# RWKV's recurrence on the whole array for two heads at once, compression weights in two halves, and another order of layer B's score products

## The chip, the cores and the metric

The kernel runs on one core of one Trainium2 chip. The metric is the device time of one execution in microseconds. "TensorE", "VectorE", "ScalarE", "GpSimd" and "SyncE" are the core's engines; the profile calls them PE (and PEld for its weight loads), DVE, ACT, POOL and SP.

## The reference, cut to what matters

Two blocks over a sequence of 256 tokens of width 2048, all in fp32. The first block projects the normed input, mixes it in two ways (NSA attention and RWKV7), gates and projects back; the second block is a differential attention layer (layer A) and a gated linear attention layer (layer B). The three places that the change touches:

```python
def rwkv7_mixer(feat, ...):            # 16 heads of 64
    def step(state, inp):
        r_t, w_t, k_t, v_t, a_t, b_t = inp
        sa = jnp.einsum('bhij,bhj->bhi', state, a_t)
        state = (state * w_t[:, :, None, :] + sa[..., None] * b_t[:, :, None, :]
                 + v_t[..., None] * k_t[:, :, None, :])
        return state, jnp.einsum('bhij,bhj->bhi', state, r_t)
...
# in nsa_mixer: keys and values of 32-token windows, through two small matrices
kc = compress(k_cmp, cmp_pos_k, cmp_k_w1, cmp_k_w2)
vc = compress(v_cmp, cmp_pos_v, cmp_v_w1, cmp_v_w2)
...
def _gla(h, ...):                      # layer B, 4 heads, chunks of 64
    def step(state, xs):
        qi, ki, vi, ti = xs
        state = jnp.exp(ti)[..., None] * state + jnp.einsum('bchk,bchv->bhkv', ki, vi)
        return state, jnp.einsum('bchk,bhkv->bchv', qi, state)
```

## The kernel before, in words

**Big products.** `gemm` (line 476) multiplies a group of weight columns with the activations. Weights come in tiles of 512 KB (`wr`, four buffers) over SyncE's queue; `weights` (line 454) lets ScalarE make the upper half of each (`wh`) and VectorE the lower half (`wl`), both in fp32r, and TensorE runs three passes (wh with the upper and the lower half of x, wl with the upper half). These steps fill most of TensorE's time. The names of the accumulators tell the group: acc_rk, acc_v, acc_kk, acc_za, acc_q, acc_Bv and so on.

**Order.** Nothing is issued as it is written. Every operation goes to a recorder, and `Plan.schedule` (line 279) makes each engine's order ahead of time from a cost model: an operation is taken when what it needs is done and a buffer of its tag is free, and among those that can start the one that is recorded first is taken (weights first of all). Buffers of a tag go out in the order of first use. `Plan.run` (line 377) books the time, with an extra for TensorE when the array's shape changes. The order on each engine is then fixed; on the chip each engine goes through its list and waits by semaphores. All loads are issued by SyncE's queue, in order.

**RWKV.** `rwkv_group` (line 795) does four heads at once, so four groups g = 0..3; `rwkv_heads` (line 765) calls it after the products rk and v of that group. The 256 tokens are four chunks c of 64. AV and BK hold the scaled vectors, AB their products with the causal masks. The inverse of a triangular 32x32 block per head and half chunk is made by GpSimd on `blocks`, through DRAM (db, dy, dx), and completed by small products pT, pY, pX into M1. M2 holds the values in its own half of the partitions and the state in the other half. The recurrence is the loop over c near the end: pU = M1 times M2, copied by ScalarE to AVt; pS = BKt times AVt, from which VectorE makes the next state in M2; yp = AB times AVt, for c > 0 plus RT times M2. Chunk c uses partitions 0 to 63 or 64 to 127 by its parity (`own`), the state comes from the other half (`oth`). Each is one product a head:

```python
for h in range(4):
    mm(pu[own, h], M1[rows, h, c], M2[rows, c, h], ...)
```

so each writes 64 partitions, and the array is used as 128\*64 (or 64\*64 for c = 0 and for RT). An fp32 product is two MATMUL instructions in the profile. yp of all chunks stays in one PSUM bank until the group norm reads it (`bn_stats`).

**Compression.** `compress` (line 1137) is a generator that `weights` moves on by one step after each weight tile of rk2 and v2: for keys and values (kind) it loads w1 in four parts of 512 KB (tag t4, shared with many others) and runs eight products per part into ph, with 32 output partitions each, four column places in turn (128\*32).

**NSA.** `nsa_group` (line 1187) keeps probabilities of the compressed keys in pc4, two tiles a group of four heads.

**Layer B.** `gla_scores` (line 1570) makes, per head, decayed keys d (tile kd) and k2, scaled queries q1 and q2, and the scores in pB: per j of two, six products of 64 output partitions (128\*64) and then one of 128 (128\*128) from k2 and q2. The second half of k2 is a copy that GpSimd makes. VectorE also does the rest of the scaling, the upper and lower halves ATB of the scores and the wl tiles of the big product Bv that runs meanwhile (`layer_b`, line 1461).

Of the kernel before, what the change touches and what calls it, by code (L numbers as in the profile page):

```python
# [423 lines left out]
class Kernel:  # L424
# [8 lines left out]
    BUFS = {"t1": 6, "t2": 10, "t4": 5, "tiny": 24, "rtiny": 12, "rt4": 4, "rt2": 2, "rt1": 2, "rt8": 1}  # L433
# [361 lines left out]
    def rwkv_group(self, g, twd, fr, fk, fv):  # L795
# [82 lines left out]
        RT = self.sb(f"RT{g}", [128, 2, 4, 64], "rt2")  # L878
        for i in range(2):
            for o in range(2):  # L880
                S.activation(RT[hf(o), :, i:4:2, :].rearrange("p c j t -> p j c t"), AV[hf(i), :, 1 - o:4:2, 2, :], AF.Copy)

# [6 lines left out]
        AB = (self.work if g % 2 else self.big).tile([128, 4, 4, 2, 64], F32, name=f"AB{g}", tag="ml")  # L889
        for j in range(2):  # L890

            ps = [self.ps(f"pA{g}{2 * j + i}", (128, 4, 128)) for i in range(2)]
            for c in range(4):
                for i in range(2):
                    mm(ps[i][:, c], BK[hf(i), j, c].rearrange("p a t -> p (a t)"), AV[hf(i), j, c, c % 2:3:2 - c % 2, :],
                       start=(c == 0), stop=True, skip_group_check=True)
            for i in range(2):
                V.tensor_tensor(AB[:, 2 * j + i].rearrange("p c k t -> p c (k t)"), ps[i],
                                cst[:, None, C_SI:C_SI + 128].to_broadcast([128, 4, 128]), op=OP.mult)
# [5 lines left out]
        db = self.dram.tile([4, 4, 2, 32, 32], F32, name=f"db{g}")  # L905
        for q, c1, d in quads:
            nc.sync.dma_start(db[q].rearrange("h c s t -> s h c t"), AB[qp(q), :, c1:4:2, 0, 32 * d:32 * d + 32])
        Y, X = self.blocks[gp, 0], self.blocks[gp, 1]
        nc.sync.dma_start(Y, db.rearrange("q h c s t -> (q h c) s t"))
# [9 lines left out]
        dy = self.dram.tile([4, 4, 2, 32, 32], F32, name=f"dy{g}")  # L919
        nc.sync.dma_start(dy.rearrange("q h c s t -> (q h c) s t"), Y)  # L920
        dx = self.dram.tile([4, 4, 2, 32, 32], F32, name=f"dx{g}")
        nc.sync.dma_start(dx.rearrange("q h c s t -> (q h c) s t"), X)

# [17 lines left out]
        for c, c1, c2, h in units:  # L941
            mm(pv[hf(c1), c2, h], AB[hf(1 - c1), h, c, 0], AVt[hf(1 - c1), c, h], start=(c2 == 0 and h == 0), stop=True, skip_group_check=True)
# [5 lines left out]
        X = self.sb(f"X{g}", [128, 4, 2, 32], "t1", bufs=2)  # L948
        for q, c1, d in quads:
            nc.sync.dma_start(M1[qp(q), :, c1:4:2, 32 * d:32 * d + 32], dy[q].rearrange("h c s t -> s h c t"))  # L950
            if d == 0:
                nc.sync.dma_start(X[qp(q)], dx[q].rearrange("h c s t -> s h c t"))
            else:
                G.memset(M1[qp(q), :, c1:4:2, 0:32], 0.0)
# [3 lines left out]
        for c, c1, c2, h in units:  # L958
            lo, hi = qp(2 * c1), qp(2 * c1 + 1)
            mm(pt[hi, c2, h], AB[lo, h, c, 0, 32:64], X[lo, h, c2], start=(c2 == 0 and h == 0), stop=True, skip_group_check=True)  # L960
# [3 lines left out]
        for c, c1, c2, h in units:  # L964
            lo, hi = qp(2 * c1), qp(2 * c1 + 1)
            mm(py[lo, c2, h], Tm[hi, c2, h], M1[hi, h, c, 32:64], start=(c2 == 0 and h == 0), stop=True, skip_group_check=True)
        for c1 in range(2):
            S.activation(M1[qp(2 * c1), :, c1:4:2, 32:64].rearrange("p h c t -> p c h t"), py[qp(2 * c1)], AF.Copy)
        pt = self.ps(f"pX{g}", (128, 2, 4, 64))
        for c, c1, c2, h in units:  # L970
            mm(pt[hf(1 - c1), c2, h], AVt[hf(c1), c, h], M1[hf(c1), h, c], start=(c2 == 0 and h == 0), stop=True, skip_group_check=True)
        for c1 in range(2):
            S.activation(M1[hf(1 - c1), :, c1:4:2].rearrange("p h c t -> p c h t"), pt[hf(1 - c1)], AF.Copy)


        yp = self.ps(f"yp{g}", U3)
        for c in range(4):
            c1, c2 = c % 2, c // 2
            own, oth = hf(c1), hf(1 - c1)
            rows = slice(0, 128) if c else own  # L980
            pu = self.ps(f"pU{g}{c}", (128, 4, 64))
            for h in range(4):
                mm(pu[own, h], M1[rows, h, c], M2[rows, c, h], start=(h == 0), stop=True, skip_group_check=True)
            S.activation(AVt[own, c], pu[own], AF.Copy)
            if c < 3:
                pS = self.ps(f"pS{g}{c}", (128, 4, 64))
                for h in range(4):
                    mm(pS[own, h], BKt[:, c, h], AVt[:, c, h], start=(h == 0), stop=True, skip_group_check=True)
                pc = PC[own, c].rearrange("p j i -> p (j i)")[:, :, None].to_broadcast([64, 4, 64])
                Sn = M2[own, c + 1]  # L990
                if c:
                    V.tensor_tensor(Sn, pS[own], M2[oth, c], op=OP.add)
                    V.tensor_tensor(Sn, Sn, pc, op=OP.mult)
                else:
                    V.tensor_tensor(Sn, pS[own], pc, op=OP.mult)
            for h in range(4):
                o = yp[own, c2 * 4 + h]
# [694 lines left out]
```

## Time and profile before

| | us |
|---|---|
| runs of the kernel before | 1483.18, 1483.45, 1488.77 |
| median | 1483.45 |
| the profiled execution, its own time | 1483.21 |
| its span, first to last instruction | 1481.4 |
| mean granted TensorE clock | 0.995 |

The profile is of one execution. A row of a timeline gives the start, the duration, the engine and what is written and read; instructions of one kind in a row are put together with their count. The ends of matmuls are modelled and they overlap, so the text goes by distances from start to start. "Idle before <- releaser" says for how long the engine stood before this instruction and what ended that.

### The profile page before, as it was taken

Reading aid. Unit: us, or ns where it says so; the run is one execution under the profiler, and the core shown is the slowest. Engines: PE = TensorE matmul, PEld = TensorE weight load, DVE = VectorE, ACT = ScalarE, POOL = GpSimd, SP = SyncE. Lnnn points to the kernel's source line nnn. Section 1 sums busy time; section 2 is a strip of 40 time slices with the busy share of each in tenths; the row PEclk is TensorE's granted clock in tenths of the full one; section 3 lists DMA queues with packets and bytes.
Section 4 is the critical chain, followed back from the end, with each engine's and each line's share of the span. In section 5 each row is a group of like instructions: output and inputs, shape, how many; then the busy total and the mean of one; then the engine's idle time right before and its main releaser. Section 6 shows DMA issues by size and latency. Waiting matters only on the chain.

```text
span 1481.4 us, 24543 instructions
## 1 busy us (share of the span) xinstructions
PE 1454.8 (98%) x9437; PEld 1278.9 (86%) x9437; DVE 967.3 (65%) x1678; ACT 768.4 (52%) x1269; POOL 316.4 (21%) x402
## 2 busy tenths in 40 slices
PE   8999999999999999999999999999999998999998
PEld 8988889989999988788888888788888897988887
DVE  5876575575857754876767676656765567565554
ACT  6542345344545544757575757554544473455532
POOL 0258846615600000030404050100100001000000
PEclk9999999999999999999999999999999999999999
DMA  9545434636524567665556566556665553655564
GB/s 334 182 131 198 160 97 139 194 104 183 156 82 148 165 218 228 212 190 174 182 171 185 167 180 215 174 186 197 205 208 186 173 172 110 222 174 185 185 213 128
DMA packets 91957, 263.42 MB, mean 178 GB/s; under 512 B 19960, under 2 KB 26512, under 8 KB 91840
## 3 DMA queue, kind: packets, MB, share of 16 engines
q1 hardware_dynamic: 91840, 261.86, 56.6%
q8 instruction: 74, 1.21, 0.3%
q14 instruction: 43, 0.35, 0.1%
HBM read 253.92 MB, written 7.90 MB: 177 GB/s over the span
## 4 chain that ended last, share of the span: by engine, by line
PE 90%; DVE 6%; issue 1%; ACT 1%; DMA 1%; POOL 1%; SPq 0%; DVEq 0%; ACTq 0%
PE acc_Bo L277 6%; PE acc_Aq L277 6%; PE acc_Ao L277 6%; PE acc_o L277 6%; PE acc_Ak L277 6%; PE acc_Av L277 6%; PE acc_rk L277 6%; PE acc_Bg L277 6%; PE acc_Ag L277 5%; PE acc_Bv L277 5%; PE acc_zb L277 3%; PE acc_Bq L277 3%; PE acc_q L277 3%; PE acc_Bk L277 3%; PE acc_v L277 3%; PE acc_za L277 2%
## 5 line engine op out<-in xcount | busy, mean ns | idle before, releaser
L277 PE MATMUL acc_rk<-xp,wh_rk 128*128 128x256 f32 x512 | 96.7, 289 | 1.3 <-ACT wh_rk L277 1.3
L277 PE MATMUL acc_Bo<-mBp,wh_Bo 128*128 128x512 f32 x256 | 89.7, 396 | 0.0
L277 POOL TENSOR_TENSOR bt<-blocks 32x30 f32<-32x30 f32 (+14 forms) x120 | 87.5, 729 | 9.0
L277 PE MATMUL acc_Ao<-mAp,wh_Ao 128*128 128x512 f32 x256 | 89.3, 395 | 0.0
L277 PE MATMUL acc_Bv<-wh_Bv,xBp 128*128 128x412 f32 (+1 forms) x320 | 88.3, 355 | 0.0
L277 PE MATMUL acc_Aq<-wh_Aq,xAp 128*128 128x512 f32 x256 | 86.0, 407 | 0.7 <-ACT xAp L277 0.7
L277 PEld LDWEIGHTS acc_rk<-xp,wh_rk 128*128 128x128 f32 x512 | 80.6, 193 | 4.9 <-issue 2.6
L277 POOL TENSOR_TENSOR blocks<-blocks,bt 32x30 f32<-32x30 f32 (+14 forms) x120 | 80.8, 673 | 9.3
L277 PE MATMUL acc_Ag<-wh_Ag,xAp 128*128 128x512 f32 x256 | 81.6, 395 | 0.0
L277 PE MATMUL acc_Ak<-wh_Ak,xAp 128*128 128x512 f32 x256 | 80.8, 392 | 0.0
L277 PE MATMUL acc_Av<-wh_Av,xAp 128*128 128x512 f32 x256 | 80.8, 392 | 0.0
L277 PE MATMUL acc_Bg<-wh_Bg,xBp 128*128 128x512 f32 x256 | 80.5, 393 | 0.0
L277 PE MATMUL acc_o<-wh_o,mp 128*128 128x512 f32 x256 | 79.8, 392 | 0.0
L277 PE MATMUL acc_rk<-xp,wl_rk 128*128 128x256 f32 x256 | 72.9, 286 | 0.5 <-DVE wl_rk L277 0.5
L277 PE MATMUL acc_Bo<-mBp,wl_Bo 128*128 128x256 f32 x256 | 71.1, 280 | 0.0
L277 PE MATMUL acc_Ao<-mAp,wl_Ao 128*128 128x256 f32 x256 | 70.9, 279 | 0.0
L277 DVE TENSOR_TENSOR wl_o<-wr_o,wh_o 128x1024 fp32r<-128x1024 f32 x32 | 39.2, 1225 | 38.2 <-ACT wh_o L277 38.0
L277 DVE TENSOR_TENSOR wl_Bo<-wr_Bo,wh_Bo 128x1024 fp32r<-128x1024 f32 x32 | 39.2, 1224 | 36.0 <-ACT wh_Bo L277 36.0
L277 DVE TENSOR_TENSOR wl_Bg<-wr_Bg,wh_Bg 128x1024 fp32r<-128x1024 f32 x32 | 39.2, 1225 | 33.9 <-ACT wh_Bg L277 33.9
L277 ACT ACTIVATE wh_Bo<-wr_Bo 128x1024 fp32r<-128x1024 f32 x32 | 34.0, 1062 | 51.8 <-PE acc_Bo L277 48.5
L277 PEld LDWEIGHTS acc_Bv<-wh_Bv,xBp 128*128 128x128 f32 x320 | 60.1, 190 | 0.9
L277 DVE TENSOR_TENSOR wl_rk<-wr_rk,wh_rk 128x1024 fp32r<-128x1024 f32 (+1 forms) x33 | 41.5, 1260 | 29.0 <-ACT wh_rk L277 29.0
(731 smaller groups left out, 4426.4 us busy)
## 6 DMA issues: line engine op xcount, KB each, us to landing
wr_o<-w SPq DMA_DIRECT2D x32, 512.0 KB, 3.6
wr_Aq<-w SPq DMA_DIRECT2D x32, 512.0 KB, 3.7
wr_Ak<-w SPq DMA_DIRECT2D x32, 512.0 KB, 3.7
wr_Av<-w SPq DMA_DIRECT2D x32, 512.0 KB, 3.9
wr_Ag<-w SPq DMA_DIRECT2D x32, 512.0 KB, 3.6
wr_Ao<-w SPq DMA_DIRECT2D x32, 512.0 KB, 3.8
wr_Bg<-w SPq DMA_DIRECT2D x32, 512.0 KB, 4.3
wr_Bo<-w SPq DMA_DIRECT2D x32, 512.0 KB, 3.9
```

The costliest lines, as they stand in the source:

```text
L277: op.issued = getattr(getattr(self.nc, op.eng), op.method)(*op.args, **op.kw)
```

## The change

RWKV: M1, X, AB and the DRAM tiles get an order with the heads of a chunk side by side (`at(c)` puts chunks of one parity together), so that two heads are one operand of 128 columns. pU, pS and yp become two products a chunk instead of four, with all 128 rows and 128 output partitions; of each result the two diagonal 64x64 blocks (`own2`) are taken and the others are left. For that the unused rows have to be zero: RT becomes twice as large, half of it zeroed by GpSimd, in one buffer instead of two; M2's state half for chunk 0 is zeroed. yp gets a bank per chunk, and ScalarE copies it to ys, from which the norm goes on. AB's evictions and the state updates go by halves.

Compression: w1 comes in two halves of 1 MB (two loads each) in one buffer of its own, and each half's products run from the last to the first.

Layer B: per head the twelve half-array products come first and the two whole-array ones last, with another order within each six; the copy into k2 goes to VectorE.

Others: pc4 has three buffers instead of four, the scratch for dynamic DMAs is half as large.

```diff
-"rt4": 4, "rt2": 2, ...
+"rt4": 4, "rt4z": 1, ...
...
-        RT = self.sb(f"RT{g}", [128, 2, 4, 64], "rt2")
-        for i in range(2):
-            for o in range(2):
-                S.activation(RT[hf(o), :, i:4:2, :]..., AV[hf(i), :, 1 - o:4:2, 2, :], AF.Copy)
+        RT = self.sb(f"RT{g}", [128, 4, 4, 64], "rt4z")
+        for o in range(2):
+            G.memset(RT[hf(1 - o), 1 - o:4:2], 0.0)
+            for i in range(2):
+                S.activation(RT[hf(o), 1 - o:4:2, i:4:2, :]..., AV[hf(i), :, 1 - o:4:2, 2, :], AF.Copy)
...
+        at = lambda c: c % 2 * 2 + c // 2
+        of = lambda c1: slice(2 * c1, 2 * c1 + 2)
+        AB = ....tile([128, 2, 4, 4, 64], F32, name=f"AB{g}", tag="ml")
...
             for i in range(2):
-                V.tensor_tensor(AB[:, 2 * j + i]..., ps[i], cst[:, None, C_SI:C_SI + 128]..., op=OP.mult)
+                for k in range(2):
+                    V.tensor_tensor(AB[:, k, :, 2 * j + i], ps[i][:, :, 64 * k:64 * k + 64], cst[...], op=OP.mult)
...
-        db = self.dram.tile([4, 4, 2, 32, 32], F32, name=f"db{g}")
+        db = self.dram.tile([4, 2, 4, 32, 32], F32, name=f"db{g}")
...
+        G.memset(M2[hf(1), 0], 0.0)
...
-        yp = self.ps(f"yp{g}", U3)
+        ys = self.sb(f"ys{g}", U3, "t2")
+        pair = lambda x, j: x[:, 2 * j:2 * j + 2].rearrange("p h x -> p (h x)")
+        own2 = lambda p: [(i, p[hf(i), :, hf(i)]) for i in range(2)]
         for c in range(4):
             own, oth = hf(c1), hf(1 - c1)
-            rows = slice(0, 128) if c else own
-            for h in range(4):
-                mm(pu[own, h], M1[rows, h, c], M2[rows, c, h], start=(h == 0), ...)
-            S.activation(AVt[own, c], pu[own], AF.Copy)
+            for j in range(2):
+                mm(pu[:, j], pair(M1[:, at(c)], j), pair(M2[:, c], j), start=(j == 0), ...)
+            for i, p in own2(pu):
+                S.activation(AVt[own, c, i:4:2], p, AF.Copy)
             if c < 3:
-                for h in range(4):
-                    mm(pS[own, h], BKt[:, c, h], AVt[:, c, h], start=(h == 0), ...)
+                for j in range(2):
+                    mm(pS[:, j], pair(BKt[:, c], j), pair(AVt[:, c], j), start=(j == 0), ...)
                 Sn = M2[own, c + 1]
-                if c:
-                    V.tensor_tensor(Sn, pS[own], M2[oth, c], op=OP.add)
-                    V.tensor_tensor(Sn, Sn, pc, op=OP.mult)
-                else:
-                    V.tensor_tensor(Sn, pS[own], pc, op=OP.mult)
+                for i, p in own2(pS):
+                    if c:
+                        V.tensor_tensor(Sn[:, i:4:2], p, M2[oth, c, i:4:2], op=OP.add)
+                    else:
+                        V.tensor_tensor(Sn[:, i:4:2], p, PC[own, c, :, i:i + 1]..., op=OP.mult)
+                if c:
+                    V.tensor_tensor(Sn, Sn, PC[own, c]..., op=OP.mult)
-            for h in range(4):
-                mm(yp[own, c2 * 4 + h], AB[:, h, c, 1], AVt[:, c, h], ...)
+            yp = self.ps(f"yp{g}{c}", (128, 2, 128))
+            for j in range(2):
+                mm(yp[:, j], pair(AB[:, 1, at(c)], j), pair(AVt[:, c], j), start=(j == 0), ...)
             if c:
-                for h in range(4):
-                    mm(yp[own, c2 * 4 + h], RT[oth, c2, h], M2[oth, c, h], start=False, ...)
+                for j in range(2):
+                    mm(yp[:, j], pair(RT[:, c], j), pair(M2[:, c], j), start=False, ...)
+            for i, p in own2(yp):
+                S.activation(ys[own, 4 * c2 + i:4 * c2 + 4:2], p, AF.Copy)
...
-            for part in range(4):
-                w1 = self.sb(f"w1_{kind}{part}", [128, 8, 128], "t4")
-                nc.sync.dma_start(w1, a["cw1"][kind, part])
-                for l in range(8):
-                    ll, o = part * 8 + l, l % 4 * 32
-                    mm(ph[o:o + 32], wins[kind][:, ll], w1[:, l], start=(ll < 4), stop=(ll >= 28), ...)
-                if part < 3:
-                    yield
+            for half in range(2):
+                w1 = self.sb(f"w1_{kind}{half}", [128, 2, 8, 128], "w1")
+                for part in range(2):
+                    nc.sync.dma_start(w1[:, part], a["cw1"][kind, 2 * half + part])
+                for l in reversed(range(16)):
+                    ll, o = half * 16 + l, l % 4 * 32
+                    mm(ph[o:o + 32], wins[kind][:, ll], w1[:, l // 8, l % 8], ...)
+                if half == 0:
+                    yield
...
-        pc4 = [self.sb(f"pc{g}{t}", [128, 4, 4, 32], "pc4", bufs=4) for t in range(2)]
+        pc4 = [self.sb(f"pc{g}{t}", [128, 4, 4, 32], "pc4", bufs=3) for t in range(2)]
...
-            G.tensor_copy(k2[:, :, 1], d[:, :, 1])
+            V.tensor_copy(k2[:, :, 1], d[:, :, 1])
...
             for j in range(2):
                 for i, c in enumerate((0, 2)):
                     mm(p[0:64, 2 * i, 0:64], d[:, j, c], q[:, j, c], ...)
-                    mm(p[0:64, 2 * i, 64:128], d[:, j, c], q1[:, j, i], ...)
                     mm(p[64:128, 2 * i, 64:128], d[:, j, c + 1], q[:, j, c + 1], ...)
+                    mm(p[0:64, 2 * i, 64:128], d[:, j, c], q1[:, j, i], ...)
+            for j in range(2):
                 f2 = lambda x: x[:, j].rearrange("p c t -> p (c t)")
                 mm(p[:, 1], f2(k2), f2(q2), start=False, ...)
...
-    nc = bacc.Bacc("TRN2", ..., dynamic_dma_scratch_size=1024)
+    nc = bacc.Bacc("TRN2", ..., dynamic_dma_scratch_size=512)
```

## Rows read from the trace of the kernel before

**Rows 1.** The page, part 1: busy us, share of the span, instructions.
```profile
PE 1454.8 (98%) x9437; PEld 1278.9 (86%) x9437; DVE 967.3 (65%) x1678; ACT 768.4 (52%) x1269; POOL 316.4 (21%) x402
```

**Rows 2.** Timeline of TensorE, 164 to 168 us: start, duration, what.
```profile
164.77 0.68 PE L277 MATMUL pS<-AVt,BKt 128*64 128x64 f32 x8
165.29 0.63 PE L277 MATMUL yp<-AVt,AB 128*64 128x64 f32 x8
...
166.55 0.28 PE L277 MATMUL acc_rk<-xp,wl_rk 128*128 128x256 f32 x1
166.66 0.40 PE L277 MATMUL acc_rk<-xp,wh_rk 128*128 128x256 f32 x2
166.99 0.68 PE L277 MATMUL pU<-M,M 128*64 128x64 f32 x8
...
167.82 0.40 PE L277 MATMUL acc_rk<-xp,wh_rk 128*128 128x256 f32 x2
```

**Rows 3.** Timeline of TensorE, 161 to 163 us, group 0's pX and first pU.
```profile
161.78 0.97 PE L277 MATMUL pX<-M,AVt 64*64 64x64 f32 x26
...
162.77 0.45 PE L277 MATMUL pU<-M,M 64*64 64x64 f32 x5
```

**Rows 4.** Timeline of TensorE, 692 to 694 us, layer A.
```profile
692.05 0.62 PE L277 MATMUL acc_Aq<-wh_Aq,xAp 128*128 128x512 f32 x2
...
692.73 0.62 PE L277 MATMUL acc_Aq<-wh_Aq,xAp 128*128 128x512 f32 x2
693.19 0.83 PE L277 MATMUL poA<-vA,PTA 128*128 128x128 f32 x6
...
694.09 0.63 PE L277 MATMUL acc_Aq<-wh_Aq,xAp 128*128 128x512 f32 x2
```

**Rows 5.** Timeline, all engines, 1229 to 1250 us; in brackets idle before and releaser.
```profile
1229.70 3.55 POOL L277 COPY k<-kd 128x128 f32<-128x128 f32 x1 [133.76 <-DVE kd L277]
...
1233.31 0.80 PE L277 MATMUL pB<-q,k 128*128 128x128 f32 x2 [2.94 <-POOL k L277]
...
1236.00 0.29 POOL L277 COPY k<-kd 128x128 f32<-128x128 f32 x1 [2.74 <-PE pB L277]
...
1236.43 0.50 DVE L277 CAST ATB0h<-pB 64x128 fp32r<-64x128 f32 x2 [3.32 <-ACT ATB0h L277]
...
1249.90 0.46 PE L277 MATMUL pB<-q,k 128*128 128x128 f32 x2 [0.80 <-DVE k L277]
```

**Rows 6.** Windows: stretch, us, engines' busy time (instructions), clock, DMA share, GB/s.
```profile
8.00:12.00 4.00, 2.25 (x17) 1.84 (x15) 2.15 (x5) 3.16 (x6) 0.00 (x0) 1.00 0.97 373
...
1232.00:1238.00 6.00, 4.69 (x31) 3.75 (x32) 2.62 (x8) 1.00 (x2) 1.55 (x2) 0.55 0.24 70
1238.00:1244.00 6.00, 6.00 (x44) 5.27 (x44) 4.87 (x13) 2.16 (x4) 0.29 (x1) 0.88 0.25 70
```

**Rows 7.** Timeline of TensorE, 220 to 222 us, group 1, chunk 1.
```profile
220.71 0.68 PE L277 MATMUL yp<-M,RT 64*64 64x64 f32 x8
221.31 0.39 PE L277 MATMUL acc_kk<-xp,wh_kk 128*128 128x256 f32 x1
```

**Rows 8.** Waits of TensorE: us in total, times, longest.
```profile
PE pU L277 <- DVE M L277: 1.1, 2, 0.7
PE ph L277 <- DMA w<-cw: 1.0, 1, 1.0
...
PE pS L277 <- ACT AVt L277: 0.3, 1, 0.3
```

**Rows 9.** Timeline of SP, ScalarE and TensorE, 10 to 21 us.
```profile
10.32 0.53 SPq L277 DMA_DIRECT2D cw<-cw  x1
11.67 0.35 SPq L277 DMA_DIRECT2D wr_rk<-w  x1
...
17.12 1.06 ACT L277 ACTIVATE wh_rk<-wr_rk 128x1024 fp32r<-128x1024 f32 x1 [1.43 <-DMA wr_rk<-w]
...
20.29 0.40 PE L277 MATMUL acc_rk<-xp,wh_rk 128*128 128x256 f32 x2
```

**Rows 10.** DMA issues, 60 to 440 us: count, KB each, median us to landing.
```profile
w<-cw SPq DMA_DIRECT2D x8, 512.0 KB, 4.8
```

More of the change, by code (lines that the diff above doesn't have):

```diff
@@ L959, in rwkv_group @@
             lo, hi = qp(2 * c1), qp(2 * c1 + 1)
-            mm(pt[hi, c2, h], AB[lo, h, c, 0, 32:64], X[lo, h, c2], start=(c2 == 0 and h == 0), stop=True, skip_group_check=True)
+            mm(pt[hi, c2, h], AB[lo, 0, at(c), h, 32:64], X[lo, c2, h], start=(c2 == 0 and h == 0), stop=True, skip_group_check=True)
         for c1 in range(2):
@@ L979, in rwkv_group @@
             own, oth = hf(c1), hf(1 - c1)
-            rows = slice(0, 128) if c else own
-            pu = self.ps(f"pU{g}{c}", (128, 4, 64))
-            for h in range(4):
-                mm(pu[own, h], M1[rows, h, c], M2[rows, c, h], start=(h == 0), stop=True, skip_group_check=True)
-            S.activation(AVt[own, c], pu[own], AF.Copy)
+            pu = self.ps(f"pU{g}{c}", (128, 2, 128))
+            for j in range(2):
+                mm(pu[:, j], pair(M1[:, at(c)], j), pair(M2[:, c], j), start=(j == 0), stop=True, skip_group_check=True)
@@ L985, in rwkv_group @@
+            for i, p in own2(pu):
+                S.activation(AVt[own, c, i:4:2], p, AF.Copy)
             if c < 3:
-                pS = self.ps(f"pS{g}{c}", (128, 4, 64))
-                for h in range(4):
-                    mm(pS[own, h], BKt[:, c, h], AVt[:, c, h], start=(h == 0), stop=True, skip_group_check=True)
-                pc = PC[own, c].rearrange("p j i -> p (j i)")[:, :, None].to_broadcast([64, 4, 64])
+                pS = self.ps(f"pS{g}{c}", (128, 2, 128))
+                for j in range(2):
+                    mm(pS[:, j], pair(BKt[:, c], j), pair(AVt[:, c], j), start=(j == 0), stop=True, skip_group_check=True)
@@ L990, in rwkv_group @@
                 Sn = M2[own, c + 1]
-                if c:
-                    V.tensor_tensor(Sn, pS[own], M2[oth, c], op=OP.add)
-                    V.tensor_tensor(Sn, Sn, pc, op=OP.mult)
-                else:
-                    V.tensor_tensor(Sn, pS[own], pc, op=OP.mult)
-            for h in range(4):
-                o = yp[own, c2 * 4 + h]
-                mm(o, AB[:, h, c, 1], AVt[:, c, h], start=(c2 == 0 and h == 0), stop=not c, skip_group_check=True)
+                for i, p in own2(pS):
+                    if c:
+                        V.tensor_tensor(Sn[:, i:4:2], p, M2[oth, c, i:4:2], op=OP.add)
+                    else:
+                        V.tensor_tensor(Sn[:, i:4:2], p, PC[own, c, :, i:i + 1].to_broadcast([64, 2, 64]), op=OP.mult)
@@ L999, in rwkv_group @@
+                if c:
+                    V.tensor_tensor(Sn, Sn, PC[own, c].rearrange("p j i -> p (j i)")[:, :, None].to_broadcast([64, 4, 64]), op=OP.mult)
+            yp = self.ps(f"yp{g}{c}", (128, 2, 128))
+            for j in range(2):
+                mm(yp[:, j], pair(AB[:, 1, at(c)], j), pair(AVt[:, c], j), start=(j == 0), stop=not c, skip_group_check=True)
             if c:
-                for h in range(4):
-                    mm(yp[own, c2 * 4 + h], RT[oth, c2, h], M2[oth, c, h], start=False, stop=True, skip_group_check=True)
+                for j in range(2):
+                    mm(yp[:, j], pair(RT[:, c], j), pair(M2[:, c], j), start=False, stop=True, skip_group_check=True)
```

64 lines of the change are left out of this document (32 added, 32 removed).

## The prediction

> **What bounds the kernel now.** I read the page first: TensorE has a matmul in flight for 98% of the span, every other engine is well below [rows 1]. So time is won or lost only where TensorE's own stream of instructions gets shorter or stops. Then I went through TensorE's timeline for the stretches that the diff touches, in steps from start to start, because the ends of matmuls are modelled. Three things stand out.
>
> First, the price of half-array batches. A step of a big product costs 0.12 us with 256 columns: two of them span 0.40 where one spans 0.28 [rows 2]. From the wh pair at 166.66 to the one at 167.82 are 1.16 us; three big steps in it (the pair and the wl behind pU) are worth 0.36, so the batch of eight pU instructions costs 0.80. Eight of this shape among their like take 0.5: pS starts at 164.77 and yp, behind it in the same shape, at 165.29 [rows 2]. The other 0.3 is the two changes of the array's shape, into the batch and out of it: 0.15 each.
>
> Second, full-array fp32 products have no such margin: from the wh pair at 692.73 to the next at 694.09 are 1.36 us; three 512-column steps (0.23 each, as from 692.05 to 692.73) leave 0.67 for six poA instructions, 0.11 each, in and out included [rows 4].
>
> Third, layer B: TensorE stops 2.94 us for a GpSimd copy that takes 3.55 us, although the next copy of the same form takes 0.29; later it stops 0.80 us for VectorE's k [rows 5]. The granted clock after the first stop is 0.55 and 0.88 of full speed in two stretches of 6 us, so it stood at the lower of its two levels (1.2 GHz of 2.4) for most of the first [rows 6].
>
> All sums stand against the profiled execution's own 1483.21 us, which is 0.24 below the median and 1.8 above its span.
>
> **RWKV, removed and added.** The code gives the batches per group: pU of chunk 0, directly behind pX; pS+yp of chunk 0; pU of chunks 1 to 3; pS+yp+RT of chunks 1 and 2; yp+RT of chunk 3. A head product is two instructions; two heads become one product of the same two, so counts halve and each costs 0.11.
> - pU, three times: 0.80 becomes 4 x 0.11 = 0.45: saves 0.35 each.
> - pS+yp of chunk 0: 0.80 and eight more at 0.5 are 1.30; eight full-array instructions are 0.90: saves 0.40.
> - RT adds 0.60 (220.71 to 221.31, with a third shape change [rows 7]) and becomes 0.45: 0.15. So pS+yp+RT, twice, saves 0.55 each, and yp+RT 0.35 + 0.15 = 0.50.
> - pU of chunk 0 loses: it stands in the same 64\*64 shape as pX and only five of its eight start behind pX [rows 3]; I put it at 0.3 now against 0.45: minus 0.15. It also begins to wait for ScalarE's copy of pX, since it now reads all 128 rows of M1.
>
> That is 1.05 + 0.40 + 1.10 + 0.50 - 0.15 = 2.9 a group, 11.6 for four. In the timeline about four of these batches touch a compression or pA batch, which keeps a shape change there: minus 0.6. **RWKV saves 11.0.** Bounds: 9 if many more such neighbours come together, 11.6 if none.
>
> Does the old form run its products side by side? pX does: 26 instructions in 0.97 us, under 0.04 each, its tiles alternating [rows 3]. pS, with all four heads in one half, starts every 0.06 [rows 2]. The Trainium skill, "TensorEngine Tiling (Array Packing)", section Theoretical Speedup, promises up to 2x for a small dimension, which speaks against giving up half-wide tiles; by it the 448 half-array instructions would cost at pX's rate some 17 us in place of 28, and the 224 new ones (25) would lose 8 of the 11. But [rows 2] show that these batches never had the overlap.
>
> New small work: two ScalarE copies for one after pU, two per chunk after yp, VectorE's sums and the AB evictions in halves, memsets of RT and M2 on GpSimd. It all lies beside big products, on engines at 65% and less [rows 1]; without that cover each of the 28 hops of the four recurrences (seven a group) would show, at about the 0.3 of the one wait of pS for ScalarE [rows 8]. The waits already there are this one and pU's for VectorE, 1.1 us in all [rows 8]. I add 0.5; bounds 0 and 28 x 0.3 = 8. RT's single buffer, three buffers for pc4 and the db/dy/dx layout (same 128-byte runs) I cost at nothing: a group's recurrence ends before the next needs RT, and the fourth pc4 tile waits for transposes of the first head group, which come before the second one's probabilities; if either cover fails, a ScalarE or GpSimd instruction starts late and shows as a wait of RT's product or of pcp. The smaller scratch size: nothing.
>
> **Compression.** Eight batches of 16 become four of 32: four times two shape changes at 0.15, **1.2 saved**. The reversed order starts with the part that lands last, so one wait stands for all; the present batches wait 1.0 once [rows 8], which I leave in.
>
> **What moves.** w1 gets a buffer of its own. Its first half (two loads of 512 KB) then waits for nothing, and the planner gives SP's queue any free load as soon as SP has none that comes earlier in the code: so it did with the cw2 load at 10.32 us, whose weights are used only in the compression [rows 9]. The two w1 loads come before it in the code, so they now fall in there, ahead of the wr_rk tile issued at 11.67 [rows 9]. The DMA engines are busy 0.97 of that stretch, at 373 GB/s [rows 6], so 1.05 MB holds back everything behind by 2.8 us. ScalarE waited 1.43 us for that tile and has its upper half at 18.18; the lower half takes a pass of VectorE more, which I put at ScalarE's 1.06; TensorE wants the tile from 20.29 on [rows 9]: slack about 1. **I charge 2.0**; bounds 0 (the load falls later) and 2.8.
>
> **Layer B.** The copy goes to VectorE, which I price at GpSimd's own 0.29 [rows 5], and the two whole-array products come after twelve others: the stop of 2.94 goes. So does the slow clock: 0.45 x 6 + 0.12 x 6 = 3.4 us of clock lost [rows 6], some 0.6 of it while TensorE still stood: 2.8. Two shape changes fewer for each of four heads: 1.2. Together 6.9. But VectorE is late next: it stood idle 3.32 us for the first head's scores [rows 5], and only about that idle time can be given back to the last k, for which TensorE waited already, less four copies: 2.2. Between 2.2 and 6.9 I take **4.0**, nearer to VectorE's end, because the last stop of the stage is VectorE's.
>
> **Sum:** 1483.2 - 11.0 - 1.2 - 4.0 + 2.0 + 0.5 = 1469.5, rounded to **1470**.
>
> **Rivals.**
> - *Layer B pays in full and the early load is hidden*: 1469.5 - 2.9 - 2.0 = 1465. For it: the clock and the stop are plain in [rows 5, 6]. Against: VectorE's late k. 0.18.
> - *The recurrence waits.* Longer hops leave TensorE idle at pU and pS: 28 hops x 0.3 = 8 us, 1478. For it: such waits exist. Against: 1.4 us in all today [rows 8], and big products are always there to fill. 0.11.
> - *The change does not do what it says*: full-array fp32 batches between big products pay the margin too, and RWKV saves nothing: 1480.5. Against it stands [rows 4]. 0.03.
> - *Slower: w1 has one buffer.* Three reloads can't start before the previous half's products end; one load takes 4.8 us from issue to landing [rows 10], its twin 1.4 more (half of the 2.8), and if each shows in full and is followed by 2.8 of slow clock, 3 x (6.2 + 2.8) = 27: 1497. It decides from about 7 us a reload on. For it: SP issues in order, so the weight tiles queue behind a reload that waits for ph. Against: the planner places ph after the landing it expects and fills with big products; eight such loads made TensorE wait once [rows 8]. 0.04. The Trainium skill, "Trainium Kernel Development and Optimization", section Best Practices, says to double-buffer so that loads overlap compute; by that rule this rival is what one buffer brings. The trace shows overlap of another kind, other products in between.
>
> **Numbers.** The forecast has 0.64. Range: the low end is 1483.2 - 11.0 - 1.2 - 6.9 = 1464 with nothing given back, the high end 1483.2 - 9 - 1.2 - 2.2 + 2.8 + 3 = 1476.6 with a third of the bound on waits; one more on each side for a list schedule that is made anew: 1463 to 1477. A measurement of this kernel can tell about 0.5%, 7.4 us, from no change. Faster by more: forecast and first rival, 0.82. Within: waits and no saving, 0.14. Slower: 0.04.
>
> **What would show it.** After: pU, pS and yp as 128\*128 with half the count, 0.11 a step and no long step beside them; four ph batches; cw loads near 10 us and a TensorE wait for wr_rk at about 20 us; no GpSimd wait in layer B and a clock of 1.0 there, a VectorE wait in its place. I am wrong if TensorE's busy steps shrink by less than 8 us between 160 and 435, if ph stops for loads by over 3 us, or if layer B's stage keeps its length.

## The result, and the profile after

The kernel after takes 1468.26 us (median of 4, 1466.98 to 1468.6) against 1484.65 beside it: ratio 0.9883, interval 0.987 to 0.9896. A second series on another chip gave 1468.08 against 1484.12, ratio 0.9889 (0.9872 to 0.9907). So the change takes off 1.1 to 1.2%, 16 to 17 us; 13.2 were forecast (1470 from the 1483.21 of the profiled execution). Between the two profiled executions it is 14.7 us (1468.47, span 1466.7).

The page, part 1, of the kernel after: busy us, share of the span, instructions; [rows 1] before.

```profile
PE 1440.0 (98%) x9213; PEld 1273.2 (87%) x9213; DVE 971.0 (66%) x1710; ACT 779.7 (53%) x1317; POOL 319.3 (22%) x410
```

TensorE lost 224 instructions, those of the halved head products, and 14.8 us of busy time. ScalarE gained 48 small copies and 11 us, VectorE 32 instructions and 4 us. The bound is where it was: TensorE is busy 98% of the span.

**RWKV.** TensorE's timeline after, group 0's first pS and yp, then group 1's first pU: start, duration, what.

```profile
172.42 0.28 PE L277 MATMUL acc_v<-xp,wl_v 128*128 128x256 f32 x1
172.54 0.60 PE L277 MATMUL pS<-AVt,BKt 128*128 128x128 f32 x4
172.98 0.61 PE L277 MATMUL yp<-AVt,AB 128*128 128x128 f32 x4
173.34 0.48 PE L277 MATMUL acc_v<-xp,wh_v 128*128 128x256 f32 x2
173.66 0.28 PE L277 MATMUL acc_v<-xp,wl_v 128*128 128x256 f32 x1
...
225.34 0.28 PE L277 MATMUL acc_kk<-xp,wl_kk 128*128 128x256 f32 x1
225.46 0.60 PE L277 MATMUL pU<-M,M 128*128 128x128 f32 x4
225.82 0.48 PE L277 MATMUL acc_kk<-xp,wh_kk 128*128 128x256 f32 x2
226.14 0.28 PE L277 MATMUL acc_kk<-xp,wl_kk 128*128 128x256 f32 x1
```

Read from start to start, as in [rows 2]. From the wl at 225.34 to the next at 226.14 are 0.80 us; three big steps are worth 0.36, so pU costs 0.44, where it cost 0.80. pS and yp: 172.42 to 173.66 are 1.24, less 0.36 is 0.88, where they cost 1.30. There is no long step on either side.

**Layer B.** The timeline after, VectorE's copy and the whole-array products of the first two heads; then windows (the columns of [rows 6]).

```profile
1221.96 0.22 DVE L277 COPY k<-kd 128x128 f32<-128x128 f32 x1
...
1222.78 0.71 PE L277 MATMUL pB<-q,k 128*128 128x128 f32 x4
...
1227.94 0.22 DVE L277 COPY k<-kd 128x128 f32<-128x128 f32 x1
...
1228.22 0.71 PE L277 MATMUL pB<-q,k 128*128 128x128 f32 x4 [0.22 <-DVE k L277]
```

```profile
1224.00:1230.00 6.00, 5.78 (x49) 4.93 (x48) 5.90 (x17) 2.11 (x4) 0.00 (x0) 1.00 0.46 137
1230.00:1236.00 6.00, 5.71 (x31) 5.29 (x29) 5.25 (x13) 4.44 (x10) 0.00 (x0) 1.00 0.24 78
1236.00:1242.00 6.00, 5.18 (x64) 4.78 (x64) 5.90 (x15) 0.99 (x2) 0.00 (x0) 1.00 0.69 186
```

The stop of 2.94 and the clock of 0.55 and 0.88 [rows 5, 6] are gone; GpSimd does nothing here, and VectorE, busy 5.90 of 6 us, is next.

**Where the 14.7 us lie.** I set the starts of the same weight products of the two traces side by side. At 20 us the kernel after is 1.5 us *behind*; at the end of the first block (acc_zb, 445 us before) 7.3 ahead; at layer B's value product 8.0; at its gate product 14.3; at the end 14.7. So layer B gave 6.3, and the first block 7.3 where 9.7 was forecast. The lists of waits tell a part of what it lost; TensorE after, 60 to 440 us: us in total, times, longest; some of those of before are in [rows 8].

```profile
PE pnb L277 <- DVE sq L277: 4.1, 1, 4.1
PE ph L277 <- DMA w<-cw: 2.1, 2, 1.7
PE pT L277 <- DMA X<-dx: 1.8, 2, 1.6
PE po L277 <- DVE ys L277: 1.2, 1, 1.2
```

Summed over the stretch they are 11.7 us, before 9.2: 2.5 more; pnb was 3.2 in all before. The other loss is the clock, in the ramp and behind stops. The windows from 0 to the first product of the output projection (acc_o), before, after, and in runs 4 and 6 below:

```profile
0.00:506.58 506.58, 492.80 (x4518) 460.84 (x4518) 339.15 (x713) 239.85 (x444) 214.60 (x325) 1.00 0.51 162
0.00:499.31 499.31, 483.04 (x4293) 459.65 (x4294) 342.48 (x741) 251.16 (x492) 225.01 (x337) 0.99 0.52 164
0.00:504.93 504.93, 485.98 (x4294) 459.94 (x4295) 344.64 (x741) 250.43 (x492) 222.63 (x337) 0.99 0.52 162
0.00:518.09 518.09, 500.40 (x4357) 472.13 (x4358) 343.39 (x741) 250.64 (x492) 221.69 (x337) 0.98 0.50 158
```

Length less TensorE's busy time is its idle time: 13.8, 16.3, 19.0 and 17.7 us. The granted clock of windows of 10 us tells for how long TensorE worked at the lower of the two levels: about 3, 9, 12 and 21 us. At that level a big step takes 0.21 us instead of 0.12 (three in 0.64 from 164.75 on in the kernel after, where the clock is 0.50), so each of these microseconds loses 0.44, and the clock cost about 1.5, 4, 5.5 and 9. What is left is an estimate of what the products cost at full clock: 491 before, 479 after, 480 in run 4, 491 in run 6. So in the first block the products became some 12 us cheaper, as forecast (11.0 + 1.2), and idle time and clock, each 2 to 3 us worse, took 5 of it back.

### The profile page after: what moved, and what is told of

Read it like the earlier page. It is cut to its first block, busy times and chain, and to the rows that moved or that the text cites. A ratio compares the mean times of both kernels' runs of the same rounds, so it can differ in the third digit from the quotient of the medians.

```text
span 1466.7 us, 24187 instructions
## 1 busy us (share of the span) xinstructions
PE 1440.0 (98%) x9213; PEld 1273.2 (87%) x9213; DVE 971.0 (66%) x1710; ACT 779.7 (53%) x1317; POOL 319.3 (22%) x410
## 3 DMA queue, kind: packets, MB, share of 16 engines
q8 instruction: 72, 1.18, 0.3%
## 4 chain that ended last, share of the span: by engine, by line
PE 87%; DVE 5%; POOL 3%; DMA 2%; issue 1%; ACT 1%; SPq 1%; DVEq 0%; ACTq 0%; POOLq 0%
PE acc_Bo L277 6%; PE acc_Ao L277 6%; PE acc_o L277 6%; PE acc_Aq L277 6%; PE acc_Ak L277 6%; PE acc_Av L277 6%; PE acc_Bg L277 6%; PE acc_Ag L277 5%; PE acc_rk L277 5%; PE acc_Bv L277 4%; PE acc_zb L277 3%; PE acc_Bk L277 3%; PE acc_Bq L277 3%; PE acc_q L277 3%; PE acc_v L277 3%; PE acc_za L277 2%
## 5 line engine op out<-in xcount | busy, mean ns | idle before, releaser
L277 POOL TENSOR_TENSOR bt<-blocks 32x30 f32<-32x30 f32 (+14 forms) x120 | 91.0, 758 | 9.0
```

The lines of the kernel that those rows point to most:

```text
L277: op.issued = getattr(getattr(self.nc, op.eng), op.method)(*op.args, **op.kw)
```

## The experiments

Each was timed against the kernel before on the same chip. Differences in us are the ratio's distance from 1, times the time of before.

**1. Layer B alone**, in the kernel before:

```diff
-            G.tensor_copy(k2[:, :, 1], d[:, :, 1])
+            V.tensor_copy(k2[:, :, 1], d[:, :, 1])
...
-                    mm(p[0:64, 2 * i, 64:128], d[:, j, c], q1[:, j, i], start=False, **st)
-                    mm(p[64:128, 2 * i, 64:128], d[:, j, c + 1], q[:, j, c + 1], start=(i == 0 and j == 0), **st)
+                    mm(p[64:128, 2 * i, 64:128], d[:, j, c + 1], q[:, j, c + 1], start=(i == 0 and j == 0), **st(j))
+                    mm(p[0:64, 2 * i, 64:128], d[:, j, c], q1[:, j, i], start=False, **st(j))
+            for j in range(2):
...
-                mm(p[:, 1], f2(k2), f2(q2), start=False, **st)
+                mm(p[:, 1], f2(k2), f2(q2), start=False, **st(j))
```

> The kernel before with the change of layer B's score step alone (the copy of the second key plane on VectorE, the whole-array products last). The theory after the comparison of the two traces, in which layer B began to gain at its first score step and ended 6.5 us further ahead: the whole 6.5 us belong to this part, time about 1477 us; no wait of TensorE for GpSimd after 1200 us, granted clock 1.00 in every stretch of layer B. The rival, the prediction's own term of -4.0 (VectorE, which is the busiest engine there, gives 2.9 back): 1479.5. A third, that part of the 6.5 comes from the arrival of layer B in another phase of the clock because the kernel ahead of it is shorter: under 3 us, 1480.5 or more.

1478.78 us against 1485.24, ratio 0.9959 (0.9947 to 0.9971): 6.1 us, interval 4.3 to 7.9. In its trace nothing moves up to 1214 us, and the stage ends 6.2 to 6.3 ahead. TensorE's waits there, 1215 to 1255 us, are VectorE's alone:

```profile
PE pB L277 <- DVE kd L277: 2.0, 2, 1.1
PE acc_Bv L277 <- DVE wl_Bv L277: 0.7, 1, 0.7
PE pB L277 <- DVE k L277: 0.4, 2, 0.2
```

The same stretch of the kernel before has 2.9 for GpSimd and 0.9, 0.8 and 0.7 for VectorE. So VectorE's part rose from 2.4 to 3.1 us: it took back 0.7, and the part pays nearly in full. The last head's k, for which the kernel before waited 0.80 [rows 5], shows why. VectorE, then TensorE, in this run:

```profile
1250.25 0.22 DVE L277 COPY k<-kd 128x128 f32<-128x128 f32 x1
1250.52 0.71 PE L277 MATMUL pB<-q,k 128*128 128x128 f32 x4 [0.21 <-DVE k L277]
```

That k came no earlier: its first step starts at 1250.04, before at 1249.46. TensorE still waits less for it, since it now has 325 instructions of the value product (acc_Bv) in front of it instead of 293. From the first product of acc_Bv to the first of acc_Bg the stage takes 104.9 us instead of 111.2. Of these 6.3, idle time is 2.2 (5.4 to 3.2), the lower clock level 2.7 (6.2 us of it before, none now), and the changes of shape are left with about 1.3. The rival at 4.0 lies just outside the interval, the third theory (under 3) well outside.

**2. The copy alone, and 3. the order alone**: the first two lines of that diff, and the rest of it.

> The kernel before with the copy of the second key plane moved from GpSimd to VectorE and nothing else; the whole-array products stay where they were, between the small ones. Theory (the GpSimd copy of 3.55 us and the clock that fell behind it are the greater part): -5.2 us, time about 1478; TensorE still changes shape four times more in each score step, some 1.2 us over two heads, so it stays 1.2 behind the run with both edits. The rival (the order is what matters, because whole-array products that wait early hold all the others up): most of the gain is missing, under 2 us, 1481.5 or more.

> The kernel before with the whole-array products last and the copy left on GpSimd. Theory: the copy takes 3.55 us from about the moment the keys are there, the small products ahead of it last only some 1.5 us, so TensorE still waits about 2 us for GpSimd and the clock still falls; -1.5 to -2.5 us, time about 1481. The rival (order alone hides the copy): no wait for GpSimd over 0.5 us, clock 1.00, -5 us or more, 1478.

The copy: 1480.1, ratio 0.9969 (0.9959 to 0.9979), 4.6 us; its trace gains 4.9 to 5.0 in the stage, as the theory has it, and the rival (under 2) falls. The order: 1483.09, ratio 0.9985 (0.9977 to 0.9994), 2.2 us. What TensorE's timeline and the window behind show with the order alone:

```profile
1235.15 0.28 PE L277 MATMUL pB<-q,kd 128*64 128x64 f32 x2
1237.51 0.71 PE L277 MATMUL pB<-q,k 128*128 128x128 f32 x4 [2.08 <-POOL k L277]
```

```profile
1236.00:1242.00 6.00, 4.49 (x35) 4.05 (x36) 4.46 (x13) 1.38 (x2) 1.74 (x2) 0.74 0.28 92
```

The stop is 0.9 shorter (2.94 became 2.08), but the copy itself took 3.16 here instead of 3.55, so the small products ahead cover about 0.5 of it. Run 3's rival falls. The two edits add up to 6.8, the pair gave 6.1: by the intervals that is no difference.

**4. The recurrence alone**: the kernel before with the new rwkv_group, its buffer classes, and the sizes that make room. The core of it:

```diff
-            pu = self.ps(f"pU{g}{c}", (128, 4, 64))
-            for h in range(4):
-                mm(pu[own, h], M1[rows, h, c], M2[rows, c, h], start=(h == 0), stop=True, skip_group_check=True)
+            pu = self.ps(f"pU{g}{c}", (128, 2, 128))
+            for j in range(2):
+                mm(pu[:, j], pair(M1[:, at(c)], j), pair(M2[:, c], j), start=(j == 0), stop=True, skip_group_check=True)
```

> The kernel before with the recurrence of the kernel after alone (two heads at once on the whole array, with the tile layouts, buffers and the sizes of the decay tiles and of the scratch ring that it needs); compression and layer B stay. Theory: -10 us, time about 1473, made of some 64 changes of shape at 0.15 us each and the halved counts of products. The rival (the waits that the trace after shows ahead of the products of norm, of compression and of the recurrence, 2.5 us more between 60 and 440 us than before, belong to this part and not to the compression): -7.5, about 1475.5, with the waits for norm and score tiles at their lengths of the kernel after.

1481.37 us, ratio 0.9975 (0.9964 to 0.9986): 3.7 us, interval 2.1 to 5.3. Both theories fall. Its trace has the kernel after's 9213 instructions of TensorE. From 265 to 294 us it is 5.7 us ahead of the kernel before, at 346 only 0.7 (the kernel after 2.2 and 4.0). In between, TensorE's timeline and the windows:

```profile
298.19 1.24 PE L277 MATMUL pT<-X,AB 32*32 32x32 f32 x32 [3.25 <-DMA X<-dx]
```

```profile
296.00:302.00 6.00, 3.81 (x62) 2.90 (x64) 2.25 (x5) 2.12 (x6) 0.00 (x0) 0.59 0.97 325
302.00:308.00 6.00, 6.00 (x68) 5.65 (x63) 5.50 (x13) 3.51 (x9) 2.20 (x6) 0.55 0.14 47
```

pT needs a block X that GpSimd works out and two DMAs carry over. Its elimination ends with a copy at 290.7 us here, at 286.1 in the kernel after; SP issues X's loads at 293.61 and at 288.93. So TensorE stops 3.25 us, and then the clock is at its lower level for most of 12 us. All waits of 60 to 440 us are 14.9 us (before 9.2). By the account above the products are about 11 us cheaper, as forecast; idle time (5.2 more) and the lower clock (4 more) took 9 of it, a good part of that at this stop.

**5. The recurrence and the compression together**, that is the kernel after with layer B's old lines:

> The kernel after with layer B's score step as it was before (copy on GpSimd, the old order); recurrence and compression of the kernel after stay. The parts alone gave -6.1 us (layer B), -3.7 (recurrence) and -0.1 (compression), which makes 10 of the 17 us. Theory A (the recurrence brings its 10 us once nothing stops TensorE behind it; alone it met a stop of 3.25 us at 295 us and its low clock, which its neighbour, the compression, changes): the layer-B part is additive, the time is 6 us above the kernel after, 1474 to 1475. Theory B (the parts help each other in layer B, by the phase of the clock there): 1478 or more.

1475.77 us, ratio 0.9938 (0.9923 to 0.9953): 9.2 us, interval 7.0 to 11.4. The same chip had the kernel after at 1468.08, so layer B is worth 7.7 here by the medians, a microsecond over theory A's 6 and 2 us below where B begins. Between its trace and run 9's, with nearly the same clock (0.997 and 0.996), it is 5.5 us, 1473.28 against 1467.81, and the stage itself takes 111.0 us against 104.9, 6.1 more: A. Its trace has no stop at 295 us, and in layer B it has the old 2.9 us for GpSimd again. So the recurrence's gain does come once that stop is absent; alone it met the stop by the new list order.

**6. The changes of shape put back**: the kernel after, with a product of one column on a quarter of the array behind each pU and each yp, 32 in all, into a slot that nothing reads.

```diff
-            pu = self.ps(f"pU{g}{c}", (128, 2, 128))
+            pu = self.ps(f"pU{g}{c}", (128, 3, 128))
...
+            mm(pu[0:64, 2, 0:1], M1[0:64, at(c), 0], M2[0:64, c, 0, 0:1], start=False, stop=True, skip_group_check=True)
...
+            mm(yp[0:64, 2, 0:1], AB[0:64, 1, at(c), 0], AVt[0:64, c, 0, 0:1], start=False, stop=True, skip_group_check=True)
```

> The kernel after, with one product of 64 rows by 64 columns and one moving column added behind each batch of the recurrence's pU and of its yp, 32 in all, into an unused slot of the same output tile: nothing is left out, and what is added is hardly any work but two changes of shape each. Theory (the changes of shape are the greater part of the gain): 32 products at about 0.06 us and 64 changes at 0.15 us, +11.5 us, time about 1480. The rival (the halved number of products is the gain and the change of shape is cheap): 32 products at 0.06 us and little more, +2 to +3 us, time about 1471.

1484.55 us, ratio 0.9997 (0.9983 to 1.001): the whole gain of the change is gone, 16 to 17 us more than the kernel after. The rival (+2 to +3) is out. The price in TensorE's timeline:

```profile
227.31 0.81 PE L277 MATMUL pU<-M,M 128*128 128x128 f32 x6
228.05 0.39 PE L277 MATMUL acc_kk<-xp,wl_kk 128*128 128x256 f32 x1
228.28 0.39 PE L277 MATMUL acc_kk<-xp,wh_kk 128*128 128x256 f32 x2
```

From pU to the wh are 0.97; one big step is 0.12, so pU with its one tiny product costs 0.85, where it costs 0.44 in the kernel after. 0.41 for a product of two instructions with hardly any columns; 32 of them are 13.1 us. The two instructions start 0.08 apart, which leaves about 0.165 for each change of shape: 0.15 was forecast. By the account above its products cost some 12 us more than the kernel after's, the idle time 1 more, the lower clock 5 more. So the other 3 to 4 us of the run are the clock: the two of its runs with a mean clock of 0.997 and 0.998 took 1482.49 and 1480.63, 12 to 14 us more than the kernel after.

**7. The compression alone**, in the kernel before:

```diff
-            for part in range(4):
-                w1 = self.sb(f"w1_{kind}{part}", [128, 8, 128], "t4")
-                nc.sync.dma_start(w1, a["cw1"][kind, part])
+            for half in range(2):
+                w1 = self.sb(f"w1_{kind}{half}", [128, 2, 8, 128], "w1")
+                for part in range(2):
+                    nc.sync.dma_start(w1[:, part], a["cw1"][kind, 2 * half + part])
```

> The kernel before with the compression of the kernel after alone (weights by halves, one buffer of two parts, the products in the reverse order, and the smaller decay tiles and scratch ring that make room). Prediction's term: -1.2 us for the waits and shapes it takes away and +2.0 for the early load. Theory now: -1.2, +1.5 in the ramp and +1 for the wait of the second kind for its weights, time about 1484.5, no difference that can be told. The rival (the ramp's 1.5 us is no matter of this load): 1482 to 1483, and a granted clock of 1.00 in 12 to 16 us.

1485.26 us, ratio 0.9998 (0.9988 to 1.0007): no difference, as the theory has it. (pc4's three buffers and the smaller scratch are in this run and in run 4; they have no run of their own.) The ramp of its trace, TensorE's timeline:

```profile
20.05 0.65 PE L277 MATMUL acc_rk<-xp,wh_rk 128*128 128x256 f32 x4
21.23 0.39 PE L277 MATMUL acc_rk<-xp,wl_rk 128*128 128x256 f32 x1 [0.52 <-DVE wl_rk L277]
```

There is the wait for the fifth weight tile that the prediction spoke of, through VectorE's split, and it costs 0.7 us: 1.18 between two steps whose four products are worth 0.48. Its clock is 1.00 throughout the ramp, which was the rival's half. In the kernel after it isn't: a window of the ramp there, and the early load (start, duration of the issue):

```profile
12.00:16.00 4.00, 3.90 (x22) 3.90 (x23) 3.80 (x7) 3.39 (x6) 0.00 (x0) 0.64 1.04 374
```

```profile
10.38 1.64 SPq L277 DMA_DIRECT2D w<-cw  x2
```

The 1.5 us that the kernel after lost in the ramp are that clock of 0.64 (0.36 x 4 = 1.4). It isn't the early load's doing: the copy-alone run has no early load and 0.59 in the same 4 us, this run has the load and 1.00. And with TensorE slow, the late tile was in time, so its 0.7 doesn't show beside it. Run 9 is the same kernel with the load at 10.65 us and the clock at 1.00, and there the late tile shows: a stop of 0.47 for VectorE's half, 0.6 us lost.

**8. The weights late**: the kernel after, with

```diff
+                with nc.behind([op for op in nc.ops if op.dma][-1:]):
+                    for part in range(2):
+                        nc.sync.dma_start(w1[:, part], a["cw1"][kind, 2 * half + part])
```

> The kernel after, with the loads of the compression weights held behind the DMAs that were recorded ahead of them, so that the first half is not fetched at 10 us in front of the tile of the first layer's weights. Theory (the 1.5 us that the ramp lost come from that load): the fifth weight tile is issued at about 11.7 us instead of 13.9, the granted clock of 12 to 16 us is back at 1.00, and the time falls by 1.5 us to 1466.8. First rival (the clock fell because of the 1.33 us pause of TensorE at 9.2 us, which is there anyway): the clock of 12 to 16 us stays near 0.64 and the time is the same, 1468.3. Second rival: the half is now late for its products at 140 us, up to 2 us slower, 1470.

1471.83 us, ratio 0.9909 (0.9894 to 0.9924): not faster, by the ratio 3.9 us more than the kernel after, whose interval it touches. The first half is issued at 108 us. The ramp is better (0.7 us *ahead* of the kernel before at 20 us, the clock at 1.00), so as far as the trace goes the theory holds there, but ph waits 3.9 us for its weights, the clock is 0.75 from 150 to 170 and 0.59 from 300 to 310 behind a stop of 1.36 for X. Up to acc_o its idle time is 15.0 us, less than the kernel after's 16.3; what it lost is the clock, some 25 us at the lower level against 9. The second rival holds in direction.

**9 to 12. Two stops taken on.** TensorE's longest stop in the first block is pnb's. The timeline after, GpSimd and TensorE:

```profile
102.89 3.89 POOL L277 TENSOR_TENSOR bt<-blocks 32x168 f32<-32x168 f32 x1
...
107.80 2.62 POOL L277 TENSOR_TENSOR ni<-n,mhalf 128x8 f32<-128x8 f32 x1
...
111.26 0.66 PE L277 MATMUL pnb<-cst,sq 128*128 128x128 f32 x4 [4.11 <-DVE sq L277]
```

ni, the power behind the key norm, is late on GpSimd, and pnb stands at a fixed place in TensorE's order. The planner's model says 1.62 us for ni. Run 9 is the kernel after once more, on the same chip as two of the next three. Run 10 raises ni's planned cost (a), run 11 holds the compression's first half behind the decay weights at some 48 us (b), run 12 does both. Run 11 was made last, with the results of the others known.

```diff
-            return 300 + 165 * n
+            return 300 + 165 * n + 3000 * (n == 8 and "ni" == out.tensor.name[:2])
```

```diff
+                with nc.behind([op for op in nc.ops if op.dma and op.args[0].tensor.name.startswith("wa")][-1:]):
+                    for part in range(2):
+                        nc.sync.dma_start(w1[:, part], a["cw1"][kind, 2 * half + part])
```

Run 9, the kernel after:

> The kernel after itself, once more on the chip of the next three, so that these are compared with it under one roof. Theory: 1468 to 1469 us, ratio 0.988; in runs whose granted clock is lower, up to 1472.

1468.08 us, ratio 0.9889 (0.9872 to 0.9907), as expected. Run 10, edit (a):

> The kernel after, with one number of the planner changed: the power function of the key norm on GpSimd is planned 3.0 us longer, since the trace after has its 2.62 us behind a GpSimd instruction of 3.89 us and TensorE waits 4.1 us for its product pnb at 107 us. Nothing of the computation changes, the planner puts other products ahead of pnb. Theory: the wait of 4.1 us and the low clock behind it (0.72 to 0.83 for some 10 us, 1.7 to 3 us) are gone, other places change by a microsecond, 1463 to 1465 us. The rival (the planner only moves the wait to the next thing that needs GpSimd or the norm, as the transposes behind it): 1468 or more, with a wait of 2 us and more in 100 to 130 us.

1466.8 us, ratio 0.9877 (0.9861 to 0.9893): not to be told from the kernel after. pnb waits no longer; others do. Its largest waits, 60 to 440 us:

```profile
PE pT L277 <- DMA X<-dx: 2.0, 2, 1.0
PE pU L277 <- DVE M L277: 1.5, 1, 1.5
PE ph L277 <- DMA w<-cw: 1.4, 1, 1.4
```

All its waits there sum to 10.0 us against 11.7, and the clock falls to 0.81 to 0.85 in three stretches between 180 and 220 us, behind pU's stop, among others. The wait moved, though not to where the rival had it. Run 11, edit (b):

> The kernel after with the compression weights' first half held behind the loads of the decay weights at 51 us, and the planner's cost of the norm's power as it was. The run with both edits took 1461.6, the one with the norm alone 1466.8, the kernel after 1468.1. Theory A (the two edits add up; the load is worth 5 us by the ramp's late tile and by the phase of what follows): 1463. Theory B (the two need each other: the load in the middle only helps where the norm's wait does not put a low clock behind it): 1466.5 or more, with a wait of 2.8 us or more for the norm's product at 105 to 110 us.

1467.62 us, ratio 0.9893 (0.9876 to 0.9909): nothing gained. In its trace pnb stops TensorE 2.80 us, ph 3.4 in two. Theory B. Run 12, both:

> The kernel after with the planned cost of the norm's power raised by 3.0 us, and the compression weights' first half held behind the loads of the decay weights at 51 us, so that it comes neither in the first layer's ramp at 10 us nor as late as 108 us. Theory: as the run with the norm alone, less 0.7 us for the fifth weight tile of the ramp, whose split the trace with the compression alone has 0.52 us late at 20 us: 1462.5 to 1464.5. The rival (the ramp has no microsecond to give back, and the half's load of 4.8 us at 51 us delays weight tiles there instead): equal to the run with the norm alone or above it.

1461.63 us, ratio 0.9846 (0.9831 to 0.9862), an interval that lies below that of the kernel after on the same chip: 22.9 us off the kernel before, 6 more than the change brings, and a little under the 1462.5 to 1464.5 of its theory. Its largest waits, 60 to 440 us:

```profile
PE pT L277 <- DMA X<-dx: 4.3, 1, 4.3
PE pnb L277 <- DVE sq L277: 1.3, 1, 1.3
PE pa L277 <- DVE e L277: 1.1, 3, 0.6
```

8.5 us in all; ph waits 0.2 in all, and after 60 us the clock falls once only (0.66 from 160 to 170 us, behind pT's 4.3). That is a version faster than either kernel. That it has fewer stops and a higher clock is shown; that *these* two edits had to go together for a reason isn't: each makes the planner's list anew, and where the stops then fall was not foreseen in any of the runs 4, 8, 10 and 12.

## Why the prediction was right, step by step

The time fell inside the range, 1.7 us below the forecast, and the likeliest case was the one that came, with a part of a rival in it. That the sum came so near is partly luck: layer B gave 2.2 more than its term and the early load cost 1.3 less, while TensorE's waits rose 2.0 more than the 0.5 charged and the lower clock in the first block took 1 to 3 us that stood in no term.

- **RWKV, 11.0.** Right in mechanism and in price: pU 0.44 (forecast 0.45), pS and yp 0.88 (0.90), a change of shape 0.165 (0.15). Recurrence and compression together measured 9.2 (7.0 to 11.4), forecast 9.7 (11.0 + 1.2 - 2.0 - 0.5). By the account of the first block the recurrence alone (run 4) made the products about 11 us cheaper.
- **The skill's rule.** The Trainium skill, "TensorEngine Tiling (Array Packing)", section Theoretical Speedup, promises up to 2x where a dimension is 64 or less. The trace doesn't agree for these batches: by [rows 2] pU's eight half-wide instructions take 0.5 us without their borders, the four full ones 0.44 with theirs, and run 6 has a batch of another shape pay 0.33 us to come and go. The measurement decides.
- **Waits of the recurrence, +0.5.** Mis-sized, and in the wrong place. In the kernel after the hops inside the recurrence cost nothing that shows: pU's waits fell from 1.1 to 0.4 us, pS's vanished. (In other lists they show a little: pU 1.8 in run 4, 1.5 in run 10.) What rose were waits of other things that the same list orders: pnb 3.2 to 4.1, ph 1.0 to 2.1, po 1.2 new. 2.5 us more in all in the kernel after, 5.7 in the recurrence alone. The rival "the recurrence waits" had about the right size for run 4, and the wrong wait.
- **Compression, -1.2, and the early load, +2.0.** The load fell in where the prediction put it, at 10.38 us, and the tile came late by VectorE's split. The charge was too high: 0.7 us in run 7. The slack of about 1 was right, the delay wasn't: ScalarE began that tile's upper half 1.74 us later (18.86 against 17.12 [rows 9]), where the 2.8 of two whole loads were charged. In the profiled execution of the kernel after not even 0.7 shows, since the clock made TensorE later than the tile; in run 9's it does (0.6). That clock was in no step.
- **Layer B, 4.0.** The step that failed. Stop, clock and shapes were put together as 6.9, and then 2.9 taken off since VectorE, next to last, would be late. Runs 1 to 3 have 6.1 to 6.3 for the pair and 0.7 us of VectorE's lateness (2.4 to 3.1). The error was the cap: the prediction let TensorE gain only as much as VectorE's last k would come earlier. That k came 0.6 us later (run 1), and TensorE gained 6.2 all the same, because the products of acc_Bv moved in front of it; VectorE cost 0.7, not 2.9. "Layer B pays in full" was the rival's half that came true.
- **One buffer for w1.** Reloads made TensorE wait 2.1 us in 2, not 27; the rival's point (7 us a reload) was not reached.

## What to carry to other kernels

Price a batch of small products by what it pays at both borders, from start to start in the timeline, before counting its columns: here 0.33 us a batch was most of the gain, and a single tiny product of another shape brought it all back. When a stop is removed, how much earlier the next engine can deliver is no cap on the gain while TensorE has other products to put in front: here the last k came later, and the wait for it shrank. And where a planner orders a whole block, an edit makes all its stops anew: judge a part by its rows and by a run with the other parts in place, since a part alone can meet a stop that eats half of it.

## What the runs showed of the hardware that wasn't expected

- The same GpSimd copy of 128x128 takes 3.16 to 3.56 us, 0.29, or 0.66 to 0.92 when VectorE's operations cover a part of it. In all five traces that have it on GpSimd (before, runs 3, 4, 5 and 7), the long one lies where VectorE's operations with two inputs run without a break, and ends within 0.2 us of the last of them (before: 1233.26 against 1233.11); the ones of 0.29 fall into VectorE's pauses (3.32 us before 1236.43 [rows 5]). In the first block a bt step took 3.89 us with VectorE busy all across (0.57 for the same form in the kernel before). The long one follows some 133 us in which GpSimd stood idle, but idle time alone doesn't do it: after 159 us idle a GpSimd operation on 128x1 takes 0.55 in the kernel before, and its next one, after 1.71, 0.59. That VectorE holds GpSimd up here is argued from the overlap; no run changed VectorE's work alone.
- The granted clock stood at its lower level for some microseconds behind each stop of 2.8 us and more in these traces: 0.55 behind 2.94 [rows 6], 0.72 in the 6 us behind 4.11, 0.59 and 0.55 behind 3.25. Behind stops of 1.1 to 1.4 it went either way: at 9 us of the ramp 0.64 and 0.59 behind 1.33 and 1.18, 1.00 behind 1.26 and 1.37.
- What that means for comparing single profiles: of 65 executions of the kernel before, the 9 with a mean clock of 0.993 took 1486.3 us on average, the 22 with 0.995 1484.1, the 6 with 0.997 1483.4. About 1 us a thousandth, so a single trace can be some microseconds off for a reason that no edit made.
